# Fewer weight blocks formed during the attention stage of a two-layer trunk, sums of squares taken in shorter runs, and merged outputs stored from temporaries

## The chip, the core and the metric

One core of a Trainium2 chip runs one program that computes the whole trunk once, from weights and activations in HBM to the output in HBM. The engines are TensorE (PE in the profile, with its weight loads as PEld), VectorE (DVE), ScalarE (ACT), GpSimd (POOL) and SyncE (SP), which here does nothing but issue DMAs. The metric is device time in microseconds; lower is better.

## The reference

A decoder trunk with D = 1024, a sequence of S = 1024, batch 1, two layers, all in float32. Layer 0 mixes tokens with a chunked gating MLP, layer 1 with dilated attention; each is followed by an MLP with squared ReLU (hidden width 4096), and a final RMSNorm ends it.

```python
for layer in range(DEPTH):
    y = _rms_norm(h, mix_norm_g[layer])
    if layer % 2 == 0:  y = gating_mixer(y)     # gelu(y @ w_in) -> u, v; u * (W_s LN(v) + b) @ w_out
    else:               y = dilated_attention(y)
    h = h + y
    y = _rms_norm(h, mlp_norm_g[layer])
    h = h + jnp.square(jax.nn.relu(y @ w_up[layer])) @ w_down[layer]
return _rms_norm(h, final_norm_g)
```

The attention has three dilation groups of eight heads of 64, so its qkv weight has 4608 columns. Each group gives an unnormalised numerator, a denominator and a row maximum; the three are merged head by head into `o`, and `o @ w_out` is added to h.

## The kernel before

**Arithmetic.** h is kept transposed (eight tiles of 128 x 1024, channels on partitions). TensorE multiplies in a reduced float32 format, so every operand is split (`split`, L215): ScalarE copies it to `hi` (L216), VectorE takes `lo = x - hi` (L217), and each product is three matmuls, hi·hi, hi·lo and lo·hi. The large products also use a seven-product form (Strassen's): the four blocks of 128 x 512 that make up a 2 x 2 block of weights are combined into seven blocks, and each of the seven has to be formed by additions on VectorE and then split. The seven are called `SEVEN` = 1 to 7.

**Stages.** In the time of the profile: the mixer (its v and u halves, then its output product `w_o`) up to about 302 us; the first MLP up to about 890 us; the normalised input and the value products of the attention up to 1083 us; twelve attention units up to about 1410 us; the output product of the attention, with h loaded back and added to, up to 1516 us; the second MLP and the final norm up to 2144 us. A unit of the attention is one head pair `hp` (0 to 3) with one dilation group, in the order 1, 2, 0; it multiplies q and k (`unit_qk`), scores, applies the exponential, transposes and multiplies by V. After the three units of a head pair, `merge` forms N, the merged output of that pair, in two halves.

**Who forms a unit's q and k weights.** Unit 0's are formed on the chip by GpSimd. Those of the other units are formed early by `prepare` (L476) and stored: it loads four blocks (`t<-in_w_qkv`, L177), does four additions on VectorE (L491, L492, L497, L500), and for each of seven forms a `put` makes hi on ScalarE (`tr<-r`, L216), lo on VectorE (L217) and stores both with two DMAs of 256 KB to the DRAM tile `wd` (L488); a unit reads its forms back as `wp<-wd`. `prepare` is a generator: each `yield pace` gives the number of nanoseconds, in the planner's clock, until its next piece may be put into the program. `PREPARED` says which units are formed where: units 1 to 5 in the mixer, from the moment the u tiles come to tile 4; units 6, 7, 8 and 10 in the value stage; units 9 and 11 during the attention itself, with four raw buffers of their own. `PACE` holds the pitch for each of these, 2100 ns in the mixer.

**Other weights formed early.** From q = 5 on (`OPEN`), each step of the first MLP calls `prepare_late` at three points (`LATER`), which gives 33 turns; in each, one weight block of a later stage is fetched, one is split and one is stored as a hi/lo pair `wl`. `LATE` lists 32 blocks: four `dl` 0, eight `up`, eight `bo` (the attention's output weight), eight `vt` (value weights) and four `dl` 1.

**The square.** For each RMSNorm, `Square` (L258) sums the squares of h over its eight channel tiles: ScalarE squares (L267), GpSimd adds them up in one or two partial tiles (L272), and `rms` multiplies each 128 columns of them by a column of ones (`at<-ones,t`, matmuls with 128 x 1 outputs, each of them two passes on PE) to sum over partitions. At the end of the attention two squares are taken, one for each half of the tokens, with two groups (tiles 0 to 3 and 4 to 7; the last tile stays apart), so three partial tiles, and all twelve one-column matmuls stand in a row.

**Order.** PE's order is written by hand: a planner keeps a clock `flow.t`, adds the columns of each matmul to it, and takes the next piece of a side generator (`flow.pump`) when its due time has come; the due times come from the table `LAT`. The other engines follow the order of the program, with some pieces raised in priority. Nearly all DMAs are issued by SP, in one order, so a DMA whose buffer is not free holds up those behind it.

**Buffers.** Temporaries of 128 x 512 (tags `t` for t and tr) have 13 buffers, raw loads (`r`) 4; `slot` is a pool of larger tiles, and `o` is one of them; the PSUM has three banks called mm and five called at.

**The end of the attention.** `split_N` (L1544) splits N and, for hp < 3, stores it to `od` (L1550), to be read back when the output product needs it (L1557); for hp = 3 it stays on the chip. `project` (L1592) multiplies hp 0 to 2 for all channel tiles first, starting from h and leaving the sum in h, and hp 3 last.

Of the kernel before, what the change touches and what calls it, by code (L numbers as in the profile page):

```python
# [1 line left out]

# [8 lines left out]
F32 = mybir.dt.float32  # L11
# [6 lines left out]
P = 128  # L18
# [95 lines left out]
PREPARED = ((1, 2, 3, 4, 5), (6, 7, 8, 10), (9, 11))  # L114
PACE = (2100.0, 2500.0, 1900.0, 3500.0)
LAT = dict(sum=2600.0, rms=2600.0, tile=1600.0, gate=8500.0, soft=5500.0, turn=4200.0, fe=1300.0, v=2000.0, qk=4200.0, merge=2600.0, out=700.0, fex=3.0, ve=1600.0, vd=6000.0, ex=15000.0)
# [3 lines left out]
def trunk(ctx: ExitStack, tc: tile.TileContext, xT, w_u, w_v, w_o, w_s, b_s, w_qkv, w_vt, w_bo, rel,  # L120
# [137 lines left out]
    class Square:  # L258


        def __init__(self, cols, groups=1):
            self.cols, self.acc, self.first = cols, None, range(0, KT, KT // groups)
            self.n = cols.stop - cols.start

        def add(self, k):
            sq = temp()[:, 0:self.n]
# [10 lines left out]

        def rms(self, out=None):
            ps = at_bank()
            nb = self.n // P  # L280
            for b in range(nb):
                for i, x in enumerate(self.parts):
                    matmul(ps[:, b:b + 1], x[:, blk(b)], ones[:, 0:1], passes=2, start=(i == 0),
                           stop=(i == len(self.parts) - 1))
            with tc.high_priority(offset=PRIO):
                return rsqrt(ps[:, 0:nb], 1.0 / D, out)
# [8 lines left out]
    def normed(sq, gi, out):  # L295

        r = sq.rms()
# [85 lines left out]
    class Terms:  # L383
# [8 lines left out]
        def first(self, sq, gi):  # L392

            r = sq.rms()
# [13 lines left out]
        def second(self, sq, gi):  # L408
            r = sq.rms()
# [23 lines left out]
        def second_plain(self, sq, gi):  # L433
            r = sq.rms()
# [39 lines left out]
    wd = {(i, p): dram.tile([P, 2, HALF], F32, name=f"wd{i}_{p}", bufs=1) for i in sum(PREPARED, ()) for p in SEVEN}  # L474

    def prepare(unit_list, pace, own=temp):  # L476

        tt = nc.vector.tensor_tensor
        for i in unit_list:
            n = 3 * (i // 3 * 3 + ORDER[i % 3])  # L480
            r00, r10, r01, r11 = (load(w_qkv[n + a][:, half(b)], own()) for a, b in ((0, 0), (1, 0), (0, 1), (1, 1)))
            yield max(pace, 18000.0) if own is raw else pace
# [26 lines left out]
    LATE.update({("vt", k): w_vt[0, k] for k in range(KT)})  # L509
    LATE.update({("dl", 1, a): w_dl[1, a] for a in range(4)})  # L510
    wl = {key: dram.tile([P, 2, HALF], F32, name="wl" + "_".join(map(str, key)), bufs=1) for key in LATE}
# [1246 lines left out]
```

## Time and profile before

| | |
|---|---|
| three runs | 2144.22, 2148.14, 2157.18 us; median 2148.14 |
| the profiled execution | 2146.25 us |
| its span, first to last instruction | 2144.5 us |
| mean granted TensorE clock | 0.994 |
| PE busy | 2111.6 us, 98% |
| DVE, ACT, POOL busy | 1537.3, 1168.5, 507.1 us (72, 54, 24%) |
| PE busy from 1083 to 1211 us (units 0 to 3) | 118.74 of 128 us |
| PE busy from 1211 to 1307 us | 94.68 of 96 us |
| PE busy from 1307 to 1403, 1403 to 1490 us | 94.54 of 96, 86.19 of 87 us |
| PE busy from 1490 to 1516 us (end of the attention) | 25.49 of 26 us |
| PE busy from 1516 to 2100 us (second MLP) | 583.36 of 584 us |

The profile is one execution; its span lies 1.75 us below its own time, and that is 1.89 us below the median of the three runs. A stretch in which PE is busy all the time can still be slow if the granted clock is below 1.00, so the clock is read beside the busy time. In a row of the timeline, the first two numbers are the start and the busy time of a group of like instructions, and the bracket at its end holds the idle time of that engine just before them and what ended it. Line numbers are those of the kernel before; in the kernel after, the same code stands three lines lower near the top (L216 is L219, L177 is L180, L188 is L191), and 19 to 64 lines lower further down (L488 is L507, L1550 is L1604).

### The profile page before, as it was taken

How to read it: one execution, taken by the hardware profiler on the slowest of the kernel's cores; microseconds unless marked ns; L12 is line 12 of the kernel's file. 1: busy time of each engine (PE TensorE's matmuls, PEld its weight loads, DVE VectorE, ACT ScalarE, POOL GpSimd, SP SyncE). 2: the span in 40 equal slices, each digit the busy share in tenths (PEclk: the TensorE clock that was granted, in tenths of full speed). 3: DMA queues.
4: the chain of work that ended last, by engine and by line, in shares of the span. 5: the costliest groups of instructions: out<-in, count | busy, mean ns of one | idle time of the engine just before them, and what ended most of it. 6: DMA issues, size and time to landing. Idle time of an engine off the chain costs nothing.

```text
span 2144.5 us, 30686 instructions
## 1 busy us (share of the span) xinstructions
PE 2111.6 (98%) x10192; PEld 1745.2 (81%) x10192; DVE 1537.3 (72%) x2853; ACT 1168.5 (54%) x2360; POOL 507.1 (24%) x381
## 2 busy tenths in 40 slices
PE   8999999999999999999999999999999999999997
PEld 7888888888888888888877787878888888888886
DVE  7877679665689877697357666667885555988776
ACT  7645446566665444245266666666465556544442
POOL 2000124322323332520200000002342332432244
PEclk9999999999999999999999999999999999999999
DMA  6325814578765443549786646481254443654432
GB/s 217 125 73 216 284 60 161 200 267 285 271 202 189 157 157 118 198 166 341 261 251 215 197 157 189 146 278 60 77 201 151 154 157 123 211 163 147 152 115 79
DMA packets 221875, 384.47 MB, mean 179 GB/s; under 512 B 39577, under 2 KB 67348, under 8 KB 221716
## 3 DMA queue, kind: packets, MB, share of 16 engines
q1 hardware_dynamic: 212576, 381.15, 52.0%
q10 hardware_dynamic: 9140, 1.36, 0.5%
q8 instruction: 80, 1.31, 0.2%
q14 instruction: 79, 0.65, 0.1%
HBM read 247.52 MB, written 134.91 MB: 178 GB/s over the span
## 4 chain that ended last, share of the span: by engine, by line
PE 87%; DVE 5%; DMA 4%; ACT 3%; issue 2%; POOL 0%; SPq 0%; DVEq 0%; POOLq 0%; ACTq 0%
PE mm L188 45%; PE at L188 41%; PE at L195 2%; DMA wd<-tr 1%; DMA od<-o 1%; DMA h<-in_xT 1%; DVE tr L217 0%; DMA r<-in_w_v 0%; DVE t L1678 0%; DMA V<-vd 0%; ACT t L1350 0%; ACT k L1273 0%; DVE y L217 0%; DVE k L1274 0%; DMA o<-od 0%
## 5 line engine op out<-in xcount | busy, mean ns | idle before, releaser
L216 ACT ACTIVATE wp<-r 128x512 fp32r<-128x512 f32 (+3 forms) x403 | 238.4, 597 | 345.4 <-PE at L188 213.1
L217 DVE TENSOR_TENSOR wp<-r,wp 128x512 fp32r<-128x512 f32 (+3 forms) x396 | 312.6, 794 | 147.6 <-ACT wp L216 144.6
L188 PE MATMUL mm<-t,wp 128*128 128x512 f32 x1368 | 347.9, 397 | 8.3 <-DVE k L1274 6.0
L188 PE MATMUL at<-hx,wp 128*128 128x512 f32 x1452 | 340.6, 389 | 0.6 <-DVE h L989 0.6
L188 PEld LDWEIGHTS at<-hx,wp 128*128 128x128 f32 x1452 | 272.4, 188 | 57.9 <-DVE h L989 1.1
L188 PEld LDWEIGHTS mm<-t,wp 128*128 128x128 f32 x1368 | 251.5, 189 | 62.5 <-DVE k L1274 7.5
L272 POOL TENSOR_TENSOR t<-t 128x512 f32<-128x512 f32 (+1 forms) x64 | 80.5, 1258 | 700.3 <-ACT t L267 544.6
L188 PE MATMUL at<-y,wp 128*128 128x512 f32 x1008 | 245.9, 390 | 0.0
L188 PE MATMUL mm<-hx,wp 128*128 128x512 f32 x984 | 234.4, 389 | 1.0 <-DVE hx L217 1.0
L188 PEld LDWEIGHTS at<-y,wp 128*128 128x128 f32 x1008 | 189.6, 188 | 39.8 <-issue 0.4
L188 PEld LDWEIGHTS mm<-hx,wp 128*128 128x128 f32 x984 | 184.6, 188 | 39.7 <-DVE hx L217 1.3
L188 PE MATMUL mm<-y,wp 128*128 128x512 f32 x816 | 212.7, 400 | 1.0 <-ACT t L758 0.4
L359 POOL TENSOR_TENSOR t<-r 128x512 f32<-128x512 f32 (+3 forms) x62 | 82.0, 1323 | 476.3 <-DMA r<-in_w_dn 127.0
L188 PEld LDWEIGHTS mm<-y,wp 128*128 128x128 f32 x816 | 151.3, 191 | 34.3 <-ACT t L758 1.3
L217 DVE TENSOR_TENSOR hx<-t,hx 128x512 fp32r<-128x512 f32 x192 | 164.4, 862 | 8.8 <-ACT hx L216 8.7
L188 PE MATMUL mm<-y,whi 128*128 128x512 f32 x512 | 158.2, 390 | 0.0
L216 ACT ACTIVATE hx<-t 128x512 fp32r<-128x512 f32 x192 | 118.8, 627 | 26.5 <-DMA t<-hid 22.3
L188 PE MATMUL at<-t,wp 128*128 128x512 f32 x552 | 130.6, 389 | 0.0
L361 POOL TENSOR_TENSOR r<-r 128x512 f32<-128x512 f32 (+3 forms) x62 | 90.6, 1461 | 169.1 <-DVE wp L217 156.8
L989 DVE TENSOR_TENSOR h<-h,at 128x512 f32<-128x512 f32 x144 | 97.9, 680 | 36.0 <-PE at L188 35.3
L188 PEld LDWEIGHTS at<-t,wp 128*128 128x128 f32 x552 | 103.6, 188 | 21.5
L188 PEld LDWEIGHTS mm<-y,whi 128*128 128x128 f32 x512 | 95.6, 188 | 19.6
(228 smaller groups left out, 3453.4 us busy)
## 6 DMA issues: line engine op xcount, KB each, us to landing
t<-hid SPq DMA_DIRECT2D x182, 256.0 KB, 4.1
wd<-tr SPq DMA_DIRECT2D x154, 256.0 KB, 3.0
wp<-wd SPq DMA_DIRECT2D x77, 512.0 KB, 4.4
hid<-t SPq DMA_DIRECT2D x140, 256.0 KB, 2.8
r<-in_w_up SPq DMA_DIRECT2D x120, 256.0 KB, 2.7
r<-in_w_dn SPq DMA_DIRECT2D x80, 256.0 KB, 2.5
hid<-b SPq DMA_DIRECT2D x56, 256.0 KB, 2.9
r<-in_w_v SPq DMA_DIRECT2D x48, 256.0 KB, 3.0
```

The lines of the kernel that those rows point to most:

```text
L188: nc.tensor.matmul(out, lhsT, rhs, **kw)
L195: nc.tensor.transpose(out, src, ident)
L216: nc.scalar.activation(hi, src, AF.Copy)
L217: (engine or nc.vector).tensor_tensor(lo, src, hi.bitcast(F32), op=ALU.subtract)
L272: nc.gpsimd.tensor_tensor(self.acc, self.acc, sq, op=ALU.add)
L359: tt(r3, r[0, 0], r[1, 0], op=ALU.subtract)
L361: tt(r[1, 1], r[1, 0], r[0, 0], op=ALU.subtract)
L989: return engine.tensor_tensor(hs[i, s], hs[i, s], src, op=ALU.add).ins
```

## The change

It has these parts:

1. **Where weights are formed.** The mixer now forms units 1 to 6 instead of 1 to 5, begins one u tile earlier (tile 3 instead of 4) and takes its pieces at a pitch of 1700 ns instead of 2100. The value stage forms 7, 8, 9 and 10, four units as before. Unit 11 is formed by a new generator, `prepare_apart`, in the last eight of the turns that the first MLP has. Nothing is formed during the attention.
2. **What makes room for that.** `LATE` loses `vt` 4 to 7 and `dl` 1. The four value blocks are loaded raw and split where they are used; the four `dl` 1 blocks are formed in the second MLP, which now has turns too.
3. **The square.** At the attention's end the partial tiles are now tiles 0 to 4 and 5 and 6, with the last apart; each partial tile is multiplied by the ones as soon as it is whole, in four matmuls (eight passes) at a time, the first before the last tile's square and the others with 900 ns of the planner's clock between them.
4. **Merged outputs.** For hp < 3, N is split into two temporaries, and stored with two DMAs of 256 KB instead of one of 512 KB.
5. **The output product.** The copy of a partial sum from PSUM back to h is put into the program one head pair into the next channel tile, and `LAT`'s `ex` goes from 15000 to 18000.

```diff
-PREPARED = ((1, 2, 3, 4, 5), (6, 7, 8, 10), (9, 11))
-PACE = (2100.0, 2500.0, 1900.0, 3500.0)
-LAT = dict(..., ex=15000.0)
+PREPARED = ((1, 2, 3, 4, 5, 6), (7, 8, 9, 10))
+APART = 11
+PACE = (1700.0, 2500.0, 1900.0)
+LAT = dict(..., ex=18000.0, ones=900.0)
...
         def add(self, k):
+            if k == KT - 1 and len(self.first) > 1:
+                self.total()
             sq = temp()[:, 0:self.n]
...
+        def total(self):
+            x = self.parts.pop(0)
+            last = not self.parts
+            if not self.begun:
+                self.ps = at_bank()
+            for b in range(self.n // P):
+                matmul(self.ps[:, b:b + 1], x[:, blk(b)], ones[:, 0:1], passes=2, start=not self.begun, stop=last,
+                       skip_group_check=True)
+                self.begun = True
+
+        def sums(self):
+            while len(self.parts) > 1:
+                self.total()
+                yield LAT["ones"] if self.n == HALF else 0
+            self.total()
+
         def rms(self, out=None):
-            ps = at_bank()
-            nb = self.n // P
-            for b in range(nb):
-                for i, x in enumerate(self.parts):
-                    matmul(ps[:, b:b + 1], x[:, blk(b)], ones[:, 0:1], passes=2, start=(i == 0),
-                           stop=(i == len(self.parts) - 1))
...
-    def prepare(unit_list, pace, own=temp):
+    def prepare(unit_list, pace):
...
-    LATE.update({("vt", k): w_vt[0, k] for k in range(KT)})
-    LATE.update({("dl", 1, a): w_dl[1, a] for a in range(4)})
+    LATE.update({("vt", k): w_vt[0, k] for k in range(4)})
+    LATE_DL = {("dl", 1, a): w_dl[1, a] for a in range(4)}
...
+    def prepare_apart(i):
+
+        tt = nc.vector.tensor_tensor
+        n = 3 * (i // 3 * 3 + ORDER[i % 3])
+        src = lambda a, b: w_qkv[n + a][:, half(b)]
+        put = lambda p, held: placed(wd[i, p], held)
+        r10, r11 = fetch(src(1, 0)), fetch(src(1, 1))
+        yield
+        tt(r10[1], r10[1], r11[1], op=ALU.add)
+        r00 = fetch(src(0, 0))
+        put(4, r11)
+        yield
+        x = rtemp()
+        x = x, x.bitcast(F32)
+        tt(x[1], r10[1], r00[1], op=ALU.subtract)
+        put(5, r10)
+        yield
...
-    coming_late = prepare_late()
+    coming_late = [chain(prepare_late(LATE), prepare_apart(APART)), prepare_late(LATE_DL)]
...
-        if tiles[0] == 4:
+        if tiles[0] == 3:
             flow.add(prepare(PREPARED[0], PACE[0]))
...
-                if layer == 0 and q >= OPEN and calls[0] in LATER:
+                if q >= OPEN and calls[0] in LATER:
                     save()
-                    next(coming_late, None)
+                    next(coming_late[layer], None)
...
-        t = slot((P, 2, HALF), F32R, "o")
-        N = [u for u in U if u.hp == hp and u.g == 0][0].N
-        split(t[:, 0, :], t[:, 1, :], N[:, half(i)])
+        N = [u for u in U if u.hp == hp and u.g == 0][0].N[:, half(i)]
         if hp < 3:
             od = dram.tile([P, 2, HALF], F32, name=f"od{hp}_{i}", bufs=1)
-            nc.sync.dma_start(od, t.bitcast(F32))
+            o = rtemp(), rtemp()
+            split(*o, N)
+            for e, t in enumerate(o):
+                nc.sync.dma_start(od[:, e, :], t.bitcast(F32))
             kept_outs[hp, i] = od
         else:
-            outs[hp, i] = Pair(t)
+            outs[hp, i] = Pair(slot((P, 2, HALF), F32R, "o")).split(N)
...
-                if hp == hps[0] and n + 1 < len(ms):
-                    begin(ms[n + 1])
+                if hp == hps[0]:
+                    if left:
+                        leave(*left)
+                        left = None
+                    if n + 1 < len(ms):
+                        begin(ms[n + 1])
...
-                nc.scalar.activation(h[m][:, half(i)], b, AF.Copy)
+                left = m, b
...
-    flow.add(prepare(PREPARED[2], PACE[3], raw), 20000.0)
     for i in range(NU):
         unit_qk(i)
-    sq = [Square(half(s), 2) for s in range(2)]
+    sq = [Square(half(s), (0, 5)) for s in range(2)]
```

The number of instructions of PE, DVE, ACT and POOL is the same in both programs; SP's go from 1360 to 1356.

SP, the end of the mixer: the weight loads of the output product (`r<-in_w_o`, its last half blocks), the loads of the qkv blocks (`t<-in_w_qkv`) and the stores of the formed ones (`wd_<form>_<number><-tr`). Before, where the last loads of w_o stand inside unit 4:

```order
L177 DMA r<-in_w_o 128x512
L177 DMA t<-in_w_qkv 128x512 x4
L488 DMA wd_1_133<-tr 128x512 x2
L177 DMA r<-in_w_o 128x512 x2
L488 DMA wd_6_136<-tr 128x512 x2
L488 DMA wd_5_134<-tr 128x512 x2
L177 DMA r<-in_w_up 128x512
```

After, the last of them and unit 6:

```order
L180 DMA t<-in_w_qkv 128x512 x4
L507 DMA wd_1_147<-tr 128x512 x2
L180 DMA r<-in_w_o 128x512 x3
L507 DMA wd_6_150<-tr 128x512 x2
L507 DMA wd_5_148<-tr 128x512 x2
L507 DMA wd_2_151<-tr 128x512 x2
L507 DMA wd_7_149<-tr 128x512 x2
L507 DMA wd_3_152<-tr 128x512 x2
L507 DMA wd_4_153<-tr 128x512 x2
L180 DMA r<-in_w_o 128x512
```

The last load of w_o stood ahead of unit 4's stores (but those of its first form) and of all of unit 5's; now it stands behind all stores of the last unit, which is unit 6.

ScalarE, inside an attention unit (around 1124 us in the profile before): the exponentials (L1350), the additions to N (L1388), the copies out of PSUM (L1284, L1273) and the hi halves of prepared weights (`tr<-r`). Before:

```order
L1350 ACTIVATE t,st_10661<-t,st_10661 128x128 x4
L216 ACTIVATE tr<-r 128x512
L1284 ACTIVATE t<-mm 128x512
L1350 ACTIVATE t,st_10661<-t,st_10661 128x128 x4
L216 ACTIVATE tr<-r 128x512
L1388 ACTIVATE N<-at 64x256
L1284 ACTIVATE t<-mm 128x512
L1388 ACTIVATE N<-at 64x256
```

After:

```order
L1403 ACTIVATE t,st_10690<-t,st_10690 128x128 x4
L1337 ACTIVATE t<-mm 128x512
L1403 ACTIVATE t,st_10690<-t,st_10690 128x128 x4
L1441 ACTIVATE N<-at 64x256
L1337 ACTIVATE t<-mm 128x512
L1441 ACTIVATE N<-at 64x256
```

The two `tr<-r` are gone and the rest keeps its order.

PE, the end of the attention (1485 to 1510 us before): the output product's matmuls with o, the first products of the second MLP with y, and the ones. Before:

```order
L188 MATMUL mm<-o,wp 128x512 x45
L188 MATMUL at<-ones,t 128x1 x12
L188 MATMUL mm<-o,wp 128x512 x15
L195 MATMUL at<-ident,rq 128x128 x4
L188 MATMUL mm<-o,wp 128x512 x12
```

After:

```order
L191 MATMUL mm<-o,wp 128x512 x36
L191 MATMUL at<-ones,t 128x1 x4
L191 MATMUL mm<-o,wp 128x512 x15
L191 MATMUL at<-ones,t 128x1 x4
L191 MATMUL mm<-o,wp 128x512 x6
L191 MATMUL at<-ones,t 128x1 x4
L191 MATMUL mm<-o,wp 128x512 x15
L198 MATMUL at<-ident,rq 128x128 x4
```

The run of twelve is three runs of four, with 15 and 6 wide matmuls between them; the second square, a little later, is split in the same way, with 12 and 6 between its runs.

More of the change, by code (lines that the diff above doesn't have):

```diff
@@ L1 @@
 from contextlib import ExitStack, nullcontext
+from itertools import chain
 import numpy as np
@@ L295, in normed @@
     def normed(sq, gi, out):
+        yield from sq.sums()
         r = sq.rms()
@@ L392, in first @@
         def first(self, sq, gi):
+            yield from sq.sums()
             r = sq.rms()
@@ L408, in second @@
         def second(self, sq, gi):
+            yield from sq.sums()
             r = sq.rms()
@@ L480, in prepare @@
             n = 3 * (i // 3 * 3 + ORDER[i % 3])
-            r00, r10, r01, r11 = (load(w_qkv[n + a][:, half(b)], own()) for a, b in ((0, 0), (1, 0), (0, 1), (1, 1)))
-            yield max(pace, 18000.0) if own is raw else pace
+            r00, r10, r01, r11 = (load(w_qkv[n + a][:, half(b)], temp()) for a, b in ((0, 0), (1, 0), (0, 1), (1, 1)))
+            yield pace
             def put(p, src):
@@ L1082, in value_weights @@
     def value_weights(r, place=None):
-        if r == 0:
-            return [late("vt", k) for k in range(KT)]
-        return [(place or wpair)().split(load(w_vt[r, k])) for k in range(KT)]
+        return [late("vt", k) if ("vt", k) in LATE and r == 0 else (place or wpair)().split(load(w_vt[r, k]))
+                for k in range(KT)]
     flow.add(bias_rows(), 120000.0)
@@ L1669, in final @@
     def final(sq):
+        yield from sq.sums()
         r = sq.rms()
```

45 lines of the change are left out of this document (34 added, 11 removed).

## The prediction

> **What bounds the kernel.** I read the page first, for the share of PE and the chain of work that ended last:
>
> ```profile
> span 2144.5 us, 30686 instructions
> PE 2111.6 (98%) x10192; PEld 1745.2 (81%) x10192; DVE 1537.3 (72%) x2853; ACT 1168.5 (54%) x2360; POOL 507.1 (24%) x381
> ...
> PE mm L188 45%; PE at L188 41%; PE at L195 2%; DMA wd<-tr 1%; DMA od<-o 1%; DMA h<-in_xT 1%; DVE tr L217 0%; DMA r<-in_w_v 0%; DVE t L1678 0%; DMA V<-vd 0%; ACT t L1350 0%; ACT k L1273 0%; DVE y L217 0%; DVE k L1274 0%; DMA o<-od 0%
> ```
>
> PE is the bound: it is idle for only 2144.5 - 2111.6 = 32.9 us, and the change leaves PE's instructions as many as they were. So the time can only come from PE's idle time, or from matmuls that run at less than the full granted clock. The chain names two transfers the change touches, the stores `wd<-tr` and `od<-o`. Next, busy time by stretches, to see where PE idles (mixer twice; units 0 to 3; the later units, three times; the second MLP):
>
> ```profile
> core 0: us, PE busy (x) PEld busy (x) DVE busy (x) ACT busy (x) POOL busy (x), PEclk, DMA share, GB/s
> 160.00:212.00 52.00, 52.00 (x231) 43.08 (x230) 38.93 (x119) 27.03 (x79) 0.00 (x0) 1.00 0.59 215
> 212.00:256.00 44.00, 44.00 (x196) 36.44 (x195) 31.73 (x55) 18.20 (x35) 7.33 (x5) 1.00 0.80 273
> 1083.00:1211.00 128.00, 118.74 (x734) 96.68 (x733) 84.92 (x266) 82.09 (x230) 0.00 (x0) 0.97 0.64 204
> 1211.00:1307.00 96.00, 94.68 (x602) 77.92 (x601) 64.52 (x208) 62.34 (x176) 0.00 (x0) 1.00 0.55 166
> 1307.00:1403.00 96.00, 94.54 (x601) 77.86 (x600) 64.48 (x208) 61.90 (x176) 0.00 (x0) 1.00 0.55 166
> 1403.00:1490.00 87.00, 86.19 (x518) 71.11 (x518) 56.93 (x170) 60.97 (x159) 7.03 (x5) 1.00 0.59 195
> 1516.00:2100.00 584.00, 583.36 (x2572) 482.25 (x2572) 425.95 (x575) 308.45 (x544) 199.65 (x146) 1.00 0.43 148
> ```
>
> Of the 32.9 us, 128.00 - 118.74 = 9.26 lie where units 9 and 11 are formed. In the mixer, which gets the extra work, PE has no idle time to lose, and DVE works 75% and 72%.
>
> **Step A: the stalls of forming weights in the attention.** The stores there, and the timeline around PE's three longest gaps:
>
> ```profile
> L488 SPq DMA_DIRECT2D wd<-tr x28: 319/320/510, 1102.1 to 1190.9; - x28
> ```
>
> ```profile
> 1123.86 0.69 DVE L217 TENSOR_TENSOR tr<-r,tr 128x512 fp32r<-128x512 f32 x1 [5.12 <-DMA wd<-tr]
> 1124.49 0.60 ACT L1284 ACTIVATE t<-mm 128x512 f32<-128x512 f32 x1 [3.77 <-DMA wd<-tr]
> 1125.14 0.50 PE L188 MATMUL mm<-t,wp 128*128 128x512 f32 x1 [2.32 <-ACT t L1284]
> ...
> 1138.56 0.69 DVE L491 TENSOR_TENSOR r<-r 128x512 f32<-128x512 f32 x1 [3.31 <-DMA r<-in_w_qkv]
> 1144.21 0.96 PE L188 MATMUL mm<-t,wp 128*128 128x512 f32 x3 [2.56 <-DVE k L1274]
> ...
> 1189.55 0.64 ACT L216 ACTIVATE tr<-r 128x512 fp32r<-128x512 f32 x1 [2.41 <-DMA wd<-tr]
> 1193.87 1.50 PE L188 MATMUL at<-k,q 64*128 64x128 f32 x11 [2.32 <-DVE t L1521]
> ```
>
> ACT and DVE, in order, stand behind a half that waits for a temporary to be stored, or an addition that waits for its load; PE waits for what is queued behind them. All three waiting instructions are `prepare`'s and go. Gain 2.32 + 2.56 + 2.32 = 7.2 us. Late next would be whatever holds the other 2.06 us of the stretch; ends 4.9 (the third gap, 4.3 us behind ACT's wait, may have another cause) and 9.3 us.
>
> **Step B: the clock behind those stalls.** The stretches right after each, clock in the last column but two:
>
> ```profile
> 1125.80:1129.20 3.40, 3.40 (x10) 2.62 (x9) 2.39 (x12) 2.39 (x11) 0.00 (x0) 0.50 0.78 267
> 1144.21:1147.60 3.39, 3.39 (x21) 2.72 (x21) 0.69 (x2) 0.76 (x2) 0.00 (x0) 1.00 0.20 12
> 1194.06:1197.47 3.41, 3.41 (x19) 2.79 (x17) 2.48 (x8) 2.23 (x7) 0.00 (x0) 0.50 0.55 212
> ```
>
> After two of the three, PE ran 3.4 us at a clock of 0.50, work of 1.7 us at 1.00. Gain 2 x 1.7 = 3.4 us; ends 0 and 3.4.
>
> **Step C: the ones.** The timeline's two runs of twelve, each of 24 passes:
>
> ```profile
> 1490.46 2.73 PE L188 MATMUL at<-ones,t 128*128 128x1 f32 x24
> 1505.87 3.08 PE L188 MATMUL at<-ones,t 128*128 128x1 f32 x24
> ```
>
> and the clock behind them, and behind a run of eight passes at 917 us:
>
> ```profile
> 917.00:917.79 0.79, 0.79 (x10) 0.79 (x9) 0.05 (x1) 0.00 (x0) 0.00 (x0) 1.00 0.28 106
> 917.80:921.20 3.40, 3.40 (x16) 2.70 (x17) 2.53 (x7) 1.72 (x4) 2.30 (x2) 1.00 0.40 154
> ...
> 1494.44:1497.85 3.41, 3.41 (x10) 2.66 (x9) 0.94 (x6) 0.63 (x1) 1.27 (x1) 0.50 0.00 0
> 1508.09:1514.90 6.81, 6.81 (x19) 5.49 (x19) 2.96 (x9) 0.78 (x2) 0.00 (x0) 0.50 0.00 0
> ```
>
> PE counts as busy in such a run, but 2.7 and 3.1 us of it are followed by 3.41 and 6.81 us at half clock, 0.8 us by none. Eight passes take 2.73 / 3 = 0.91 us. A wide matmul takes 134.07 / 591 = 0.2269 us, by the longest piece of the chain in the mixer:
>
> ```profile
> 147.07 134.07 PE mm L188 x591
> ```
>
> Two runs stand six wide matmuls apart, 1.36 us; if one 3.4 us stretch held both, it would hold 1.8 us of such work, less than any that dropped the clock here. I take the whole 3.41 / 2 + 6.81 / 2 = 5.1 us; ends 0 and 5.1. The same twelve matmuls stay on the path.
>
> [...]
>
> **Step D: the merged outputs.** The timeline where `split_N` waits for its `o` slot, and PE just after, at head pairs 0, 1 and 2; then the issues of `od`:
>
> ```profile
> 1216.28 0.63 ACT L216 ACTIVATE o<-N 128x512 fp32r<-128x512 f32 x1 [1.55 <-DMA od<-o]
> 1219.04 1.66 PE L188 MATMUL mm<-t,wp 128*128 128x512 f32 x6 [0.96 <-DVE k L1274]
> 1314.69 1.19 PE L188 MATMUL mm<-t,wp 128*128 128x512 f32 x4 [1.12 <-DVE k L1274]
> 1409.81 1.43 PE L188 MATMUL mm<-t,wp 128*128 128x512 f32 x5 [0.60 <-DVE k L1274]
> ```
>
> ```profile
> L1550 SPq DMA_DIRECT2D od<-o x6: 319/320/332, 1211.6 to 1408.4; - x6
> ...
> DMA to landing us min/median/max: 4.7/4.8/6.6
> ```
>
> The second half of N waits until the first is stored; the copies queued behind it on ACT, then PE, are late by 0.96 + 1.12 + 0.60 = 2.7 us. With thirteen temporaries the second half need not wait. But a store now holds two temporaries that other work wants, so I take three quarters, 2.0 us; ends 2.7 and a loss (rival 2).
>
> [...] No run here times the split; if each half took as long as the whole, the sum would not move, as only the temporaries' release hangs on it.
>
> **Step E: the mixer.** The stores there, then the loads that feed them, the additions to h by the output product, and the page's transfer rate in 40 slices:
>
> ```profile
> L488 SPq DMA_DIRECT2D wd<-tr x70: 319/327/797, 171.0 to 276.9; - x70
> ```
>
> ```profile
> L177 SPq DMA_DIRECT2D t<-in_w_qkv x20: 371/430/1088, 160.4 to 257.3; - x20
> ...
> DMA to landing us min/median/max: 2.7/4.1/5.8
> ```
>
> ```profile
> L316 DVE TENSOR_TENSOR h<-h,mm x16: 676/686/689, 218.1 to 301.4; 128x512 f32<-128x512 f32 x16
> ```
>
> ```profile
> GB/s 217 125 73 216 284 60 161 200 267 285 271 202 189 157 157 118 198 166 341 261 251 215 197 157 189 146 278 60 77 201 151 154 157 123 211 163 147 152 115 79
> ```
>
> A product of 24 matmuls takes 24 x 0.2269 = 5.44 us. Seventy stores take (276.9 - 171.0) / 70 = 1.513 us each, set by the pitch of 2100; at 1700 that is 1.225. Two products earlier (10.9 us), the first store comes at 160.1, the 84th at 160.1 + 84 x 1.225 = 263.0. On SP, in order, the last w_o load now stands behind it; it lands 4.1 us later and is split in 0.64 + 0.69 us: 268.4. PE needs it in the twelfth output product, at its second half: the first product began near 212.3 (its addition at 218.1), so 212.3 + 11 x 5.44 + 2.72 = 274.9. Six us to spare. The extra DVE work per unit, 7 halves and 4 additions of 0.69 = 7.6 us, goes from 36% of a unit's 21.2 us to 44% of 17.2, so DVE goes from 75% to about 83%. Cost 0, hidden by that slack; if it is gone, rival 1.
>
> **Edits that I cost at nothing.** `prepare_apart` takes the eight turns of eight blocks: 6 loads for 8, 14 stores for 16, 7 splits for 8, four additions more (2.8 us of DVE over three steps of some 36 us); bounds 0 and 2.8. Four `vt` splits at use, 4 x (0.64 + 0.69), beside value products that fill PE; bounds 0 and 2.4, one stall of A's size. `dl` 1 in the second MLP: four loads, eight stores, beside a PE that idles 0.6 us in 584; 0 to 2.4. The value stage forms four units as before. The copy back to h, one head pair later, shares ACT with the next tile's opening, 2 x 0.6 us within two head pairs, 6 x 0.2269 = 1.36 us: hidden, narrowly; 0 to 2.
>
> **Sum.** A 7.2 + B 3.4 + C 5.1 + D 2.0 = 17.7 us. On the profiled execution's 2146.25 that is 2128.5; that execution lies 1.9 below the median, so against the median it is 2148.1 - 17.7 = 2130.4. I say 2130.
>
> **Rivals.**
> 1. *Slower: the mixer doesn't keep pace.* If SP's order, the loads and the buffers, not the pitch, set 1.513 us a store, the 84th comes at 160.1 + 127.1 = 287.2, w_o's last block at 292.6, and PE stands 17.7 us and then 1.7 at half clock: 2130 + 19.4 = 2149.4. For it: 18 x 6 transfers of 0.262 MB in 103 us are 275 GB/s, with w_o's sixteen 316, and only one slice of the page is above that (341). Against: stretches of the mixer moved 215 and 273 with PE full. The stall begins above 1.225 + 6.5 / 84 = 1.30 us a store, eats the gain at 1.50, and loses 1% at about 1.75.
> 2. *The od stores take the place of the wd stores.* Twelve stores of 256 KB in the temporaries. If half of the six merges stall as in A and B, that is 3 x (2.3 + 1.7) and the 2.0 of D: 2130 + 14 = 2144; all six, 2156. For it: the buffers are those that A's stores held. Against: A's 28 stores (1102 to 1191 us) made three stalls; at that rate twelve, over 197 us, make 1.3.
> 3. *The clock halves for another reason* than short gaps and one-column runs, so that B and C stay, 8.5 us: 2138.5. For it: the gap that ends at 1144.21 is the longest, and 1.00 followed. Against: four drops each follow such work within one stretch. [...]
> 4. *More goes:* with DVE and ACT freer, all idle time of the units, 9.3 up to 1211 us and 1.3 + 1.5 + 0.8 = 3.6 in the three stretches behind it: 9.3 + 3.4 + 5.1 + 3.6 = 21.4, so 2148.1 - 21.4 = 2126.7, and below it where the mixer's or the end's short waits shrink too.
>
> **Chances.** The sum as it stands (2127 to 2136) 0.52; rival 1 0.14; rival 2 0.12; rival 3 0.10; rival 4 0.12. From 2122 to 2150 nine in ten are left in, with part of rivals 1 and 2 above. About 1%, 21.5 us, is what a measurement of this kernel can tell from no change: faster by it is below 2126.7, which is the most of rival 4 and a little of the sum's low end, 0.17; slower is above 2169.6, the far end of rival 1, 0.05; the same 0.78.
>
> **What would show it.** In the profile after: no `tr<-r` between 1083 and 1211 us and PE busy above 125 us of such a stretch; clock 1.00 all through the attention and behind the ones; no ACT wait for `od`; in the mixer the last `wd` store before 270 us and no PE gap near 275. Wrong if a PE gap stands before the twelfth output product, if temporaries wait for `od`, or if half clock stays behind runs of eight.

## The result, and the profile after

| | before | after |
|---|---|---|
| median of six runs | 2150.68 us (2144.22 to 2157.18) | 2132.54 us (2130.76 to 2137.84) |
| ratio | 1 | 0.9923, 95% interval 0.9897 to 0.9949 |
| the profiled execution | 2146.25 us | 2131.01 us |
| its span, granted clock | 2144.5 us, 0.994 | 2129.3 us, 0.998 |

The forecast was 2130 (2122 to 2150), within 1% the likeliest. The ratio is 0.8% below 1, on the side and of the size that was forecast. The page of the kernel after: span, PE, and the chain that ended last by line.

```profile
span 2129.3 us, 30657 instructions
PE 2102.1 (99%) x10192; PEld 1739.0 (82%) x10192; DVE 1553.2 (73%) x2853; ACT 1170.5 (55%) x2360; POOL 511.1 (24%) x381
...
PE mm L191 44%; PE at L191 41%; PE at L198 2%; DVE y L220 1%; DVE t L220 1%; DVE wp L220 1%; DMA h<-in_xT 1%; DMA r<-in_w_v 0%; DVE r L437 0%; DMA t<-in_w_qkv 0%; DVE hx L220 0%; DMA V<-vd 0%; POOL t L277 0%; DVE h L332 0%; DVE b L442 0%
```

The stores `wd<-tr` and `od<-o` are no longer among the chain's entries on the page. PE's idle time went from 32.9 to 27.2 us, and its busy time fell by 9.5 us with as many instructions. Of that, 8.5 us are the half clock: the kernel before ran 17.06 us at 0.50 ahead of its last stretches, the kernel after none. (Both end at half clock, for the last 8.4 and 10.6 us of the span, beside waits of PE of 1.90 to 2.39 us.) The same stretches as before, at the times at which the same work now stands:

```profile
160.00:212.00 52.00, 52.00 (x232) 43.05 (x231) 42.36 (x114) 29.57 (x83) 0.00 (x0) 1.00 0.81 290
212.00:256.00 44.00, 43.25 (x191) 35.51 (x190) 33.86 (x68) 17.47 (x35) 6.33 (x3) 1.00 0.81 283
1083.00:1197.00 114.00, 113.37 (x728) 93.31 (x727) 72.03 (x244) 74.82 (x217) 0.00 (x0) 1.00 0.55 163
1197.00:1292.00 95.00, 94.36 (x603) 78.02 (x602) 64.29 (x207) 61.78 (x177) 0.00 (x0) 1.00 0.57 168
1292.00:1387.00 95.00, 94.36 (x603) 78.06 (x602) 64.28 (x208) 61.66 (x175) 0.00 (x0) 1.00 0.57 168
1387.00:1474.00 87.00, 83.44 (x505) 68.35 (x504) 55.57 (x166) 59.24 (x157) 5.83 (x4) 1.00 0.57 183
1474.00:1500.00 26.00, 26.00 (x144) 22.28 (x143) 17.89 (x34) 11.40 (x19) 7.73 (x6) 1.00 0.31 102
```

Where units 9 and 11 were formed, PE idles 0.63 us instead of 9.26, and nothing runs at half clock. But the stretch from 1387 has 3.56 us of idle time, where its counterpart before had 0.81, and the mixer has 0.75 that was not there.

Both programs have 10192 matmuls on PE, in the same order but for a few at the merges and at the end of the attention. So the start of the n-th matmul can be compared, in the two profiled executions:

| work up to | n-th matmul | before, us | after, us | gained in this part |
|---|---|---|---|---|
| early mixer | 900 | 187.37 | 186.38 | 0.99 |
| end of the u products, first output products | 1200 | 255.37 | 255.42 | -1.04 |
| value products | 4857 | 1083.05 | 1083.62 | -0.52 |
| the units beside which 9 and 11 were formed | 5587 | 1211.20 | 1198.26 | 13.51 |
| later units, merges of hp 0 to 2 | 6786 | 1403.04 | 1388.27 | 1.83 |
| end of the attention, squares | 7800 | 1602.64 | 1586.44 | 1.43 |
| last products | 9900 | 2079.57 | 2063.39 | -0.02 |

The first row, and 0.94 us that the kernel after loses behind the 9900th matmul, are scatter as far as can be seen: over the thirteen profiled executions of this document, the 900th matmul starts between 185.8 and 188.5 us, and in the eleven with as many matmuls the time from the 9900th to the end goes from 64.0 to 66.2 us.

The end of the attention is the surprise: 10.24 us of half clock went there, worth 5.1 us, and only 1.4 are left. The timeline of the kernel after shows a new wait:

```profile
1462.39 0.68 DVE L1590 TENSOR_TENSOR N<-N,t 128x512 f32<-128x512 f32 x1
...
1463.10 0.63 ACT L219 ACTIVATE o<-N 128x512 fp32r<-128x512 f32 x1 [0.49 <-DVE N L1590]
...
1463.78 0.49 PE L191 MATMUL mm<-o,wp 128*128 128x512 f32 x1 [1.86 <-ACT o L219]
1464.51 1.42 PE L191 MATMUL mm<-o,wp 128*128 128x512 f32 x5 [0.23 <-DVE o L220]
...
1469.90 1.43 PE L191 MATMUL mm<-o,wp 128*128 128x512 f32 x5 [0.78 <-DVE h L332]
```

PE arrives at the output product of the last head pair before its merged output is split (1.86 and 0.23 us), and then before h is added to (0.78 us).

### The profile page after: what moved, and what is told of

The parts are those of the page before. It is cut to its first block, busy times and chain, and to the rows that moved or that the text cites. A ratio compares the mean times of both kernels' runs of the same rounds, so it can differ in the third digit from the quotient of the medians.

```text
span 2129.3 us, 30657 instructions
## 1 busy us (share of the span) xinstructions
PE 2102.1 (99%) x10192; PEld 1739.0 (82%) x10192; DVE 1553.2 (73%) x2853; ACT 1170.5 (55%) x2360; POOL 511.1 (24%) x381
## 4 chain that ended last, share of the span: by engine, by line
PE 87%; DVE 6%; DMA 3%; ACT 1%; issue 1%; POOL 1%; SPq 0%; POOLq 0%; DVEq 0%; ACTq 0%
PE mm L191 44%; PE at L191 41%; PE at L198 2%; DVE y L220 1%; DVE t L220 1%; DVE wp L220 1%; DMA h<-in_xT 1%; DMA r<-in_w_v 0%; DVE r L437 0%; DMA t<-in_w_qkv 0%; DVE hx L220 0%; DMA V<-vd 0%; POOL t L277 0%; DVE h L332 0%; DVE b L442 0%
## 5 line engine op out<-in xcount | busy, mean ns | idle before, releaser
L220 DVE TENSOR_TENSOR wp<-r,wp 128x512 fp32r<-128x512 f32 (+3 forms) x400 | 329.7, 829 | 132.8 <-ACT wp L219 130.0
```

The lines of the kernel that those rows point to most:

```text
L220: (engine or nc.vector).tensor_tensor(lo, src, hi.bitcast(F32), op=ALU.subtract)
```

## The experiments

Times are medians; the kernel before, run on the same chips, had 2146.71 (e1 to e4), 2147.22 (e5, e6, e8, e9), 2147.54 (e7, e10) and 2147.55 us (e11).

**e1: the weight forming alone.** The kernel before with parts 1 and 2 of the change, and the one line that formed units during the attention taken out:

```diff
-    flow.add(prepare(PREPARED[2], PACE[3], raw), 20000.0)
```

> The kernel before with the weight forming of the kernel after alone (units 1 to 6 in the mixer, 11 in the first MLP, none in the attention); the squares, the merged outputs' slot, the copy back to h and ex = 15000 stay as before. Theory 1 (the stalls of forming, with the half clock behind them, carry most of the change): about 13 us below the kernel before, since units 2 to 4 give back 14.4 in the two traces and the mixer and the value weights take about 1.5; the two stretches of half clock behind the runs of twelve stay, so the clock is 0.50 there. Rival: the stalls went because the merged outputs left the o slot and not because the forming left; then at most 6 us below.

Measured: 2132.81 us (2130.47 to 2139.02), ratio 0.993 (0.9913 to 0.9947), 13.9 us below. Theory 1 had 13, the rival at most 6: the rival is out. The profiled execution, at the upper end with a span of 2137.3 us, ran 13.7 us at half clock behind the two runs of twelve, and 3.4 behind a wait of 3.16 us for V. From the 5100th matmul to the 5700th (in the change's two traces 108.54 and 94.17 us) it takes 94.62.

**e2: everything but the weight forming.**

```diff
-PREPARED = ((1, 2, 3, 4, 5, 6), (7, 8, 9, 10))
-PACE = (1700.0, 2500.0, 1900.0)
+PREPARED = ((1, 2, 3, 4, 5), (6, 7, 8, 10), (9, 11))
+PACE = (2100.0, 2500.0, 1900.0, 3500.0)
...
+    flow.add(prepare(PREPARED[2], PACE[3], raw), 20000.0)
```

> The kernel before with everything of the change but the weight forming (the squares in short runs, the merged outputs in temporaries, the later copy back, ex = 18000). Theory 1: about 4 us below the kernel before: 5.1 from the clock behind the ones, 1.8 from the merged outputs, less the 2.9 us that PE now waits before the output product of the last head pair. The three stalls of 2.3 to 2.6 us at units 2 to 4 are there again. Rival (the parts need each other, od stores and wd stores fight for the same temporaries): slower than the kernel before, with waits for od in front of splits.

Measured: 2145.03 us, ratio 0.9988 (0.9978 to 0.9998): 1.7 us below, where 4 were expected. The stalls are there again in the same three places, the first behind the same stores, with 2.07, 0.97 and 2.06 us of PE's idle time where the kernel before had 2.32, 2.56 and 2.32, so the second is much shorter than expected. The timeline, and the stretch behind the first:

```profile
1124.79 0.69 DVE L217 TENSOR_TENSOR tr<-r,tr 128x512 fp32r<-128x512 f32 x1 [4.20 <-DMA wd<-tr]
1125.43 0.60 ACT L1302 ACTIVATE t<-mm 128x512 f32<-128x512 f32 x1 [2.87 <-DMA wd<-tr]
1126.08 4.39 PE L188 MATMUL mm<-t,wp 128*128 128x512 f32 x11 [2.07 <-ACT t L1302]
```

```profile
1126.79:1130.20 3.41, 3.41 (x10) 2.63 (x9) 2.35 (x12) 2.40 (x12) 0.00 (x0) 0.50 0.94 262
```

No instruction waits for `od` here. So the od stores do not fight with the wd stores (rival 2 of the prediction), and nearly the whole gain of the change hangs on the weight forming. The expectation's 4 us had two wrong prices: 5.1 us for the ones, which e3, e5 and e7 put at less, and 2.9 us for the waits of the last head pair, which e4 puts at 3.9.

**e3: all twelve ones of a square in one run again.**

```diff
-            if k == KT - 1 and len(self.first) > 1:
-                self.total()
...
-            while len(self.parts) > 1:
-                self.total()
-                yield LAT["ones"] if self.n == HALF else 0
-            self.total()
+            yield 0
+            while self.parts:
+                self.total()
```

> The kernel after with all twelve one-column matmuls of each square at the attention's end in one run again. Theory 1: the clock falls to 0.50 behind one or both runs, for 3.4 to 6.8 us each, so 1.7 to 5.1 us more than the kernel after. Rival (the clock's gate looks for idle time alone, so one-column matmuls don't matter and the drops of before had another cause): clock 1.00 behind both, and the time of the kernel after.

Measured: 2133.56 us (2130.23 to 2139.49), ratio 0.9932 (0.9914 to 0.9949), against 0.9923 of the kernel after. The profile had what theory 1 did not expect, runs of 2.73 us with the full clock behind them:

```profile
1481.57 2.73 PE L191 MATMUL at<-ones,t 128*128 128x1 f32 x24
1495.32 2.73 PE L191 MATMUL at<-ones,t 128*128 128x1 f32 x24
```

```profile
1486.19:1489.60 3.41, 3.41 (x19) 2.81 (x18) 2.41 (x6) 1.23 (x3) 0.57 (x2) 1.00 0.00 0
...
1499.84:1503.26 3.42, 3.42 (x18) 2.83 (x17) 2.60 (x7) 0.31 (x1) 0.00 (x0) 1.00 0.02 5
```

The clock's changes explain it. In each execution they all lie on one grid of 3.413 us (in this one 49.18 and 2121.07, 607 steps apart). Here the grid's lines at 1482.78 and 1496.43 cut both runs in two, 1.21 and 1.53, 1.11 and 1.62 us. In the kernel before, the lines at 1491.02 and 1508.09 left 2.17 and 2.22 us in one stretch. From this came theory 2, below.

**e4: ex back at 15000,** in the kernel after, nothing else.

```diff
-LAT = dict(..., ex=18000.0, ones=900.0)
+LAT = dict(..., ex=15000.0, ones=900.0)
```

> The kernel after with LAT's ex back at 15000, nothing else. In the program's order PE then has 15 wide matmuls and two groups of four transposes where the kernel after has 12 and 8, as before. Theory 1 (the later due time put the last merge's two halves together and left PE without work, 1.86 + 0.23 + 0.78 us): these gaps go, about 2.9 us less than the kernel after. Rival (the gaps come from the copy back to h, which is one head pair later): they stay, and the time is that of the kernel after, or more where the earlier merge waits elsewhere.

Measured: 2128.88 us (2127.18 to 2131.27), ratio 0.9907 (0.9891 to 0.9923), 3.7 us below the kernel after by the medians; the intervals of the two ratios overlap. The profile tells it more sharply. The stretch that had 83.44 us of PE's work:

```profile
1387.00:1474.00 87.00, 85.50 (x522) 70.96 (x521) 55.93 (x168) 59.69 (x158) 7.14 (x5) 1.00 0.56 183
```

Between 1412 and 1480 us PE waits for nothing. From the 7150th to the 7700th matmul it takes 112.8 us, the kernel after 116.8, with no half clock in either: 3.9 us. The wait of 1.86 us stands in all four profiled executions with 18000 (the kernel after, e2, e3, e8) and in none of the nine with 15000. The rival (the copy back to h) stays as it is in both and is out.

**e5: ex = 15000 and the ones in one run,** e3's edit on e4's.

> The kernel after with ex = 15000 and with all twelve one-column matmuls of each square at the attention's end in one run. It stands against the kernel with ex = 15000 alone (2128.9 us). Theory 2, formed from the traces so far (in each of six profiled executions the clock changes only on a grid of 3.413 us, and it was halved for a stretch whose predecessor held over about 1.7 us of gaps and one-column matmuls, 2.07 and more, and not where it held up to 1.62): a run of 2.73 us puts over 1.7 us into one stretch in about 8 of 10 positions of the grid, so this kernel takes 1.7 to 3.4 us more for each run where it does, on average 2 to 4 us more than with ex = 15000 alone, with more scatter, and in its profile each run's longer part decides: over 1.7 us, 0.50 behind it; under 1.6 us, 1.00. Rival (one-column matmuls don't count, drops come otherwise): no difference, and drops that don't fit the grid.

Measured: 2128.97 us (2126.75 to 2131.28), ratio 0.9917 (0.9898 to 0.9936). By the medians there is no difference to e4; the 2 to 4 us that were expected on average did not come. The two runs of its profiled execution, and the stretch behind each:

```profile
1474.53 2.73 PE L191 MATMUL at<-ones,t 128*128 128x1 f32 x24
1489.88 2.73 PE L191 MATMUL at<-ones,t 128*128 128x1 f32 x24
```

```profile
1477.65:1481.06 3.41, 3.41 (x9) 2.64 (x8) 1.46 (x6) 1.06 (x2) 1.79 (x2) 0.50 0.00 1
...
1494.72:1498.13 3.41, 3.41 (x19) 2.82 (x18) 2.59 (x6) 0.63 (x1) 0.00 (x0) 1.00 0.02 5
```

The first run lies whole in one stretch and is followed by 3.41 us at 0.50. The second is cut into 1.43 and 1.30 us, and the clock holds. So in both runs the place on the grid decided, as theory 2 says, and its average was too high.

**e6: the o slot and the single store,** on e4.

```diff
-            o = rtemp(), rtemp()
-            split(*o, N)
-            for e, t in enumerate(o):
-                nc.sync.dma_start(od[:, e, :], t.bitcast(F32))
+            nc.sync.dma_start(od, t.bitcast(F32))
```

with `t = slot((P, 2, HALF), F32R, "o")` split ahead of it.

> The kernel after with ex = 15000 and with each merged output split into the o slot and stored by one DMA of 512 KB, as in the kernel before. Against ex = 15000 alone (2128.9 us). The prediction's step D: the waits for od come back, 2.0 us more, up to 2.7. Rival, from the run with the weight forming alone (whose three waits there were 0.63, 0.84 and 0.91 us) and the kernel after (0.63 three times, another wait in the same place): the temporaries are worth some 0.5 us only.

Measured: 2131.47 us (2128.61 to 2134.75), ratio 0.9925 (0.9909 to 0.9942), 2.6 us above e4 by the medians. ACT's wait at the first merge in its timeline, then PE's waits in the units (us in total, times, longest), in e6 and in e4:

```profile
1202.86 0.63 ACT L219 ACTIVATE o<-N 128x512 fp32r<-128x512 f32 x1 [1.20 <-DMA od<-o]
```

```profile
PE mm L191 <- DVE k L1327: 2.0, 3, 0.9
PE at L198 <- DVE tr L220: 0.8, 3, 0.3
```

```profile
PE at L191 <- DVE t L1574: 1.9, 3, 0.6
```

From the 5100th to the 6900th matmul e6 takes 285.7 us and e4 284.0: 1.7 us, near the prediction's 2.0 and not the rival's 0.5. But it is not simply the waits that go: e4 has three others in their place, so that PE's idle time in this part is 1.91 us instead of 3.03, and 0.6 of the 1.7 us are not idle time and stay unexplained.

**e7: run lengths.**

```diff
                 d = at_bank()
+                if q < 14:
+                    for b in range(RUNS[layer][q - OPEN]):
+                        matmul(d[:, b:b + 1], h[0][:, 0:P], ones[:, 0:1], passes=2, start=True, stop=True)
                 product(d, w[5], x.t[5])
```

> The kernel after with ex = 15000, and with 18 extra runs of one-column matmuls whose results nobody reads, one in each step q = 5 to 13 of both MLPs: 4, 5, 6, 7, 8, 9, 10, 12, 14 and 7, 8, 9, 10, 5, 6, 16, 12, 6 matmuls of 0.23 us (two passes each). They add 174 x 0.23 = 40 us; not for its time but for the clock. Theory 2: on the grid of 3.413 us, a stretch runs at 0.50 exactly when the one before it held over about 1.7 us of such a run (the traces so far leave 1.70 to 2.07 open, with one drop at 1.68); so never behind runs up to 7 (1.6 us), always behind 16 (3.6 us puts 1.8 us or more into one of two stretches, or fills one), and by position between. Rival: drops don't follow the grid, or come behind a length alone.

Measured, in one execution: 2173.08 us, and the clock behind each of 18 runs (154 matmuls in all, not the 174 of the expectation). The two that lie closest to the border, with the stretch behind the one each lies in:

```profile
1655.94 2.06 PE L192 MATMUL at<-ones,h 128*128 128x1 f32 x18
1677.02 2.29 PE L192 MATMUL at<-ones,h 128*128 128x1 f32 x20
```

```profile
1658.71:1662.13 3.42, 3.42 (x17) 2.82 (x16) 0.51 (x1) 1.12 (x2) 0.69 (x1) 1.00 0.06 21
...
1679.19:1682.61 3.42, 3.42 (x10) 2.74 (x10) 0.00 (x0) 0.00 (x0) 1.27 (x1) 0.50 0.06 18
```

The line at 1679.19 leaves 2.17 us of the second run in one stretch. All 18 runs divide there: the thirteen with at most 2.06 us in a stretch kept the clock, the five with 2.17, 2.73, 2.73, 3.10 and 3.41 lost it for one stretch. For the one-column runs of this execution the border lies between 2.06 and 2.17 us of 3.413, not at theory 2's 1.7; that theory expected drops at 1.84, 1.84, 1.88 and 2.06 us, which did not come.

**e10: the same runs, 128 columns wide** (`matmul(d[:, 0:P], h[0][:, 0:P], ones, ...)`).

> The same with the extra matmuls 128 columns wide. Theory 2 as it stands (what counts as low is a matmul of one column, that is an array that loads weights and computes next to nothing): 128 columns keep the clock at 1.00 behind all runs. Rival (what counts is any float32 matmul off the large products, or the weight loads): drops as with one column.

Measured, in one execution: 2164.55 us; the clock is 1.00 behind all 18 runs. The longest of them fills a stretch:

```profile
1734.99 3.73 PE L192 MATMUL at<-ones,h 128*128 128x128 f32 x32
```

```profile
1738.72:1742.13 3.41, 3.41 (x16) 2.81 (x16) 0.00 (x0) 0.58 (x2) 0.00 (x0) 1.00 0.00 0
```

A pass takes 0.117 us with 128 columns and 0.114 with one. So a one-column matmul held PE about as long as one of 128 columns, and only one-column runs were followed by half clock (2.17 us and more in a stretch, e7), as PE's waits of 2.32 us were in the kernel before. The two kernels are 8.5 us apart, each in a single execution; five stretches of 3.413 us at half clock are worth 8.5 us.

**e8: the mixer's pitch back at 2100,** rival 1 of the prediction made to happen.

```diff
-PACE = (1700.0, 2500.0, 1900.0)
+PACE = (2100.0, 2500.0, 1900.0)
```

> The kernel after with the mixer's pitch back at 2100, nothing else: the prediction's rival 1 made to happen. Theory 1 (the pitch sets the stores, the last load of w_o stands behind them on SP): 84 stores of 1.513 us from 159.8, so the last near 287 us where the kernel after has 267.5; w_o's last block split near 292, a gap of PE of about 16 us before the twelfth output product, near 275 us, and one or two stretches of half clock; 17 to 20 us more than the kernel after, about 2150 us. Rival (the scheduler then puts the last w_o load ahead of the stores, or the loads find room): no gap, the time of the kernel after.

Measured: 2136.04 us (2134.79 to 2140.29), ratio 0.9949 (0.9932 to 0.9967), 3.5 us above the kernel after, not 17 to 20. The stores come as late as expected, but the place is another:

```profile
L507 SPq DMA_DIRECT2D wd<-tr x84: 319/327/1006, 161.3 to 290.6; - x84
```

```profile
306.62 1.62 PE L191 MATMUL mm<-y,wp 128*128 128x512 f32 x3 [2.85 <-DVE h L332]
```

```profile
306.62:316.10 9.48, 9.48 (x26) 7.78 (x27) 1.43 (x6) 0.82 (x2) 0.00 (x0) 0.50 0.00 1
```

In this program's order all w_o loads stand ahead of unit 5's stores, so no output product waits. The forming has DVE until 290.3 us, and DVE then works through what stands behind it without a break; the last addition to h comes at 305.79 us (301.47 in the kernel after), and PE idles 2.85 us and runs at half clock behind it. This execution was the slowest of the five (2140.29 us, mean clock 0.994; the others had 0.996 and 0.997), so most of the 10.2 us at half clock are probably not in the median's 3.5 us.

**e9: fewer loads ahead of the last V,** on e4: `h_load(0, range(1))` and `proj_load(0, 0)` where four blocks of h and two of the weight stood, the rest one step later.

> The kernel after with ex = 15000, and at the end of the attention one block of h and one of the output weight ahead of the last unit's V on SP instead of four and two; PE's order is the same. With ex = 15000 PE waits 1.50 us for V at 1409 us, and V took up to 9.3 us to land. If the transfers ahead of it are what holds V, 1.0 to 1.5 us less than with ex = 15000 alone, so about 2127.5; rival (V's buffer comes free too late, whatever stands ahead): no change.

Measured: 2127.55 us (2126.67 to 2129.85), ratio 0.9909 (0.9889 to 0.9928), 1.3 us below e4 by the medians. The wait in e4 that is gone:

```profile
1410.79 0.97 PE L191 MATMUL at<-tr,V 128*128 128x128 f32 x7 [1.50 <-DMA V<-vd]
```

But e5, with e4's loads, had no such wait in its profile either, so it comes and goes by itself. The gain is not shown.

**e11: wide sums.** e9 with each square's twelve matmuls in one run, against 128 columns of ones.

```diff
-                matmul(self.ps[:, b:b + 1], x[:, blk(b)], ones[:, 0:1], passes=2, start=not self.begun, stop=last,
+                matmul(self.ps[:, blk(b)], x[:, blk(b)], ones, passes=2, start=not self.begun, stop=last,
```

> The kernel of e9 (ex = 15000, loads at the attention's end later) with the twelve matmuls of each square in one run again, but against 128 columns of ones instead of one, in all norms. If what halves the clock is the one column and not the run (as the extra runs of 128 columns showed, which took 0.117 us a pass for 0.114), the clock stays 1.00 behind both runs of 24 passes at any position of the grid, and the time is that of e9, 2127.5 us, within 1.5; rival (in their place the wide ones cost time, since five banks of the PSUM are written whole and the last norms wait for them): 1 us or more above e9.

Measured: 2125.14 us (2123.40 to 2126.37), ratio 0.9898 (0.9881 to 0.9915), the fastest here, 2.4 us below e9 by the medians. The runs and the clock around them:

```profile
1473.46 2.84 PE L191 MATMUL at<-ones,t 128*128 128x128 f32 x24
1487.16 2.84 PE L191 MATMUL at<-ones,t 128*128 128x128 f32 x24
```

```profile
1473.00:1479.00 6.00, 6.00 (x40) 5.43 (x39) 3.10 (x8) 4.09 (x7) 5.13 (x4) 1.00 0.30 90
1488.00:1494.00 6.00, 6.00 (x39) 5.31 (x39) 3.29 (x11) 0.44 (x2) 0.00 (x0) 1.00 0.02 6
```

Full clock behind runs of 24 passes, as expected; but in this execution the grid's lines at 1474.61 and 1488.26 cut both runs in two, with 1.74 us at most in one stretch, and with that much one-column runs kept the clock too (up to 2.06 us in e7). So e10, whose longest run fills a stretch of 3.41 us, and not this trace, shows that wide runs keep it. That it is faster than e9, and not the same, was not expected and is not settled: in its profile the value stage takes 0.6 us less than in e9 and PE's last wait for POOL is 0.9 us shorter; the rest lies in parts that the edit doesn't touch.

## Why the prediction was right, point by point

- **A and B, 10.6 us expected, 13.5 measured.** The mechanism was right (e1, e2). PE's idle time there fell by 9.26 - 0.63 = 8.6 us, not 7.2: the 0.63 us left are at the third gap, which the prediction doubted, and the 2.06 us that it left open all went. 3.4 us came from the clock. About 1.5 us more are neither idle time nor half clock in the profile; they are there in e2 and not in e1, so they go with the forming, but what they are stays unexplained. Half clock behind the stalls went by their place on the grid: it followed two of three in the kernel before (both of 2.32 us, and not the one of 2.56 us, which a line cuts into 1.22 and 1.35), and one of the two above 2 us in e2 (2.07, not 2.06).
- **C, 5.1 us expected.** In the two profiled executions the clock's part was just that, 10.24 us at half. But this was the step that took one execution for the rule. Behind one-column runs the four executions with runs of twelve show 10.24, 13.65, 0 and 3.41 us of half clock (before, e1, e3, e5), worth 3.4 us on average. By e7's border, near 2.1 us, I estimate that a run of 2.73 us strikes in (3.41 - 2.73 + 2 x (2.73 - 2.1)) / 3.41 = 0.57 of the positions, which makes 2 x 0.57 x 1.7 = 1.9 us for two. The medians show 0.1 us between e4 and e5 and 1.0 between the kernel after and e3, within their scatter. Short runs stay right: in no execution did the clock fall from 1.00 behind a run of eight, except at the kernel's end, where 2.2 us or more of waits stand in the same stretch.
- **A term that the prediction lacked, 3.9 us lost.** It priced the copy back to h, and said nothing of ex. With ex three us later in the planner's clock, the last merge's transposes were put into PE's order eight at a time with 12 and 9 wide matmuls between, instead of four at a time with 15, and PE ran out of other work (e4).
- **D, 2.0 us expected, 1.7 measured** (e6 against e4). The waits for `od` went, but others of 0.64 us came, and part of the 1.7 us is not idle time. The od stores landed in 3.0 us (median) in two halves, 4.8 in one piece. What counted here is when the buffer is free again: nothing waited for the halves in the kernel after, and ACT waited 1.20 us for the first whole one in e6.
- **E, 0 expected, 1.0 us lost.** The mixer kept its pace, nearly: the last store is at 267.5 us (263.0 expected), the last w_o load behind it and in time. That is (267.5 - 159.8) / 84 = 1.28 us a store, not 1.225, and just inside the 1.30 at which rival 1 would have begun. But PE waits 0.75 us at 217 us for the lo half of an earlier w_o block, which stands on DVE behind the forming's additions. e8, with the slower pitch, has no loss there, so the pitch makes it: from the 900th to the 1200th matmul the three executions at 2100 (before, e2, e8) take 68.00 us, the ten at 1700 take 68.40 to 69.74.

```profile
L507 SPq DMA_DIRECT2D wd<-tr x84: 319/326/1727, 159.8 to 267.5; - x84
```

```profile
PE mm L191 <- DVE wlo L220: 0.8, 1, 0.8
```

- **What was costed at nothing** lost 0.6 us, between the 3500th and the 4200th matmul, where the four value blocks are split: 158.07 us in the kernel after and in e1, 157.43 before and 157.45 in e2. It was bounded by 2.4. e11, which splits them too, has 157.48, so the splits alone don't make it; perhaps it is the splits beside the norm's one-column runs, which was not followed. The four `dl` 1 blocks cost nothing that can be seen.
- **The sum:** 13.5 + 5.1 + 1.7 - 3.9 - 1.0 - 0.6 = 14.8 us, against 15.2 by the spans (the scatter at the two ends, +0.99 and -0.94, nearly cancels). The medians differ by 18.1 us, but those of the kernel before alone went from 2146.71 to 2150.68 between groups of executions. So 17.7 was near in part by luck: a term too small (A) stood against one that is too large on average (C) and two that were missing (ex, and the mixer's pitch).
- **Rival 1** fell as a mechanism: its place was wrong (the end of the mixer, not the twelfth product), because SP's order changes with the pitch, and its price too. **Rival 2** fell with e2. **Rival 3** fell with e7 and e10. **Rival 4** was half right, in A.

## What to carry to other kernels

Work formed early cost here what its waits held up behind them on ACT and DVE (PE then stood 2.32, 2.56 and 2.32 us), not its own time: moving it to stages where PE was full and the queues kept pace gained 13.9 us (e1). A changed due time in a planner is a change of order and has its own price, to be read from the order at the places where PE has little else to do. And a cost that one execution shows behind a run of one-column matmuls was a draw here (10.24, 13.65, 0 and 3.41 us of half clock in four executions): price it by the share of positions in which it strikes.

## What the runs showed of the hardware

- In each of the thirteen traces all changes of the granted clock lie on one grid of 3.413 us. Its place in the program differs between executions: the first run of twelve at the attention's end began 0.56 us ahead of a line in the kernel before, 1.21 in e3 and 3.12 in e5. A stretch that held 2.17 us or more of a one-column run was followed by half clock, one with up to 2.06 was not (e7). PE was busy for all 3.41 us of the one with 2.17.
- Waits of PE were followed by half clock too, and by the profile's times mostly from a lower border on. Stretches with 1.68 us (e3, at 42.3 us), 1.69, 2.09 and 2.10 (e8), 2.07 (e2) and 2.32 us (before) of them were followed by 0.50; stretches with 1.55 (before, at 2129 us) and 1.59 (e10), and the gap of 2.56 us cut into 1.22 and 1.35 (before), were not. One stretch with 1.75 us kept the clock, at 4.5 us in e10. The ends of matmuls are modelled in the profile, so why the two borders differ stays open. The same place in e8 and in e10, each with the stretch behind it:

```profile
43.04:46.45 3.41, 1.72 (x7) 0.96 (x6) 3.10 (x10) 3.38 (x6) 0.00 (x0) 1.00 0.33 105
46.45:49.87 3.42, 3.42 (x11) 2.72 (x11) 2.65 (x7) 3.40 (x7) 0.00 (x0) 0.50 0.39 125
```

```profile
42.03:45.45 3.42, 1.83 (x7) 1.17 (x8) 3.12 (x10) 3.39 (x5) 0.00 (x0) 1.00 0.38 116
45.45:48.86 3.41, 3.08 (x16) 2.28 (x14) 3.38 (x9) 3.39 (x6) 0.00 (x0) 1.00 0.33 114
```

- Once at half clock, a stretch with 0.86 to 1.02 us of one-column time kept it there (before, e1), and one with about 0.1 us did not (e7). Behind the 2.85 us gap of e8 it stayed for 10.2 us: the first of these stretches held the gap's last 0.75 us, the second a run of eight that took 1.70 us at this clock.
- Matmuls 128 columns wide did not cost the clock behind any of e10's 18 runs, not even with 3.41 us of them in one stretch, at 0.117 us a pass instead of 0.114 (e7).
